# A decoder trunk on one core: the weights of the MLPs' first products at 32 different offsets, in two buffers of their own

## The chip, the cores and the metric

The kernel runs on one core of one Trainium2 chip, as one program. The time is device microseconds of that core, the median of several executions. Five engines work side by side and meet through semaphores: TensorE (matrix products; PE in the profile, with PEld for the loading of its stationary operand), VectorE (DVE), ScalarE (ACT), GpSimd (POOL) and SyncE (SP, which issues most DMAs). A core's SBUF has 128 partitions, and an address below is a byte offset within one partition.

## The reference, cut to what matters

The program is a two-layer decoder trunk over 256 tokens with a width of 2048, in float32. Both layers have the same MLP and the same gated embedding behind it; the mixers differ (a gated delta rule in layer 0, differential attention in layer 1):

```python
for i in range(DEPTH):                                   # DEPTH = 2
    xn = rmsnorm(h, norm_mix[i])
    h = h + (gated_deltanet(xn, ...) if i < N_A else diff_attention(xn, k_shared, v_shared, ...))
    hn = rmsnorm(h, norm_mlp[i])
    h = h + jnp.square(jax.nn.relu(hn @ mlp_w1[i])) @ mlp_w2[i]      # 2048 x 8192, 8192 x 2048
    gate = jax.nn.sigmoid(rmsnorm(h, norm_ple[i]) @ ple_w_gate[i])
    h = h + (p[i] @ ple_w_proj[i]) * gate
    if i == N_A - 1:
        kv = rmsnorm(h, kv_norm) @ w_kv                  # shared keys and values
return rmsnorm(h, final_norm)
```

The change touches `hn @ mlp_w1[i]`, the first product of each MLP, and where the last norm keeps its result.

## The kernel before, in words

Every large product is made of three matmuls in place of one: the weights are split into a rounded part `hi` and a rest `lo`, the activations into `xh` and `xl`, and `hi*xh + hi*xl + lo*xh` is accumulated in PSUM.

**A chunk of weights.** `chunk` (line 117) loads 1 MB of weights, four blocks of 128 x 512, into a buffer `raw` (three of them) by one DMA of SP's queue. It then makes two half chunks of 1024 columns each: ScalarE casts `raw` to `hi` (line 131), VectorE subtracts `hi` from `raw` to get `lo` (line 132). `hi` and `lo` come from the pool `whl`, three buffers of each, 4096 bytes long, called `whi` and `wlo`. All products of the kernel share them in turn.

**Two ways to multiply.** `g1` (line 155) holds the activations still and streams 512 columns of weights past them, lines 166 to 168. `g2` (line 137) holds a 128 x 128 block of weights still and streams all 256 tokens past it, lines 150 to 152, which leaves the result transposed. A half chunk is 24 matmuls in `g2`, and a panel (512 columns of the product, eight half chunks) is 192.

**The MLP.** `mlp` (line 558) first transposes the stream (`transposed`, line 185: TensorE transposes, ScalarE writes `xh`, VectorE `xl`). Then `first(q)`, for q from 0 to 3, makes four panels with `g2`, and squares their positive part into `hidh` and `hidl` (lines 574 to 579: two halves of a panel, each an activation and a cast on ScalarE, a product and a difference on VectorE). `second(q)` multiplies these with the second weights by `g1` and adds the result to the stream. The order is first(0), first(1), second(0), first(2), second(1), first(3), second(2), second(3). Per layer that makes 16 panels of `g2`, 32 in both.

**The order of the work.** The framework plans each engine's queue when the program is built: each engine takes its instructions in one fixed order, and an instruction may be moved ahead of others where its operands are there earlier. A write into a buffer that comes round again waits for the buffer's last readers.

**Where things lie.** A pool gives its tiles addresses in the order in which their names first occur. In the kernel before, all `whi` and `wlo` begin at a multiple of 512 bytes. The activations have one tile each for `xh` and `xl`, 16896 bytes, and `xpair` (line 200) gives two views of it: `xa` begins 448 bytes past a multiple of 512 (SHIFT = 112 floats) and `xs` at the multiple itself. `g2` streams `xa` (in attention `xb`, with the same shift). The operands that `g1` holds still are `xs` (gated embedding) and `oT` (attention's output, line 717), both at a multiple of 512, `hidh` and `hidl` at 256 past it, `oh` and `ol` (the delta rule's output, line 514) at 384 past it, and `xa` at 448 past it. The pool of an MLP, `ffn0` or `ffn1`, opens at address 122112, which is 256 past a multiple of 512, with two `hidh` and two `hidl` of 16384 bytes each. It lies over the memory of the mixer's pools, which are closed by then; 187648 and on was `R1`, `o` and `kT` of the delta rule.

Of the kernel before, what the change touches and what calls it, by code (L numbers as in the profile page):

```python
# [10 lines left out]
F32 = mybir.dt.float32  # L11
F32R = mybir.dt.float32r
# [4 lines left out]
P = 128  # L17
D = 2048
T = 256
NT = T // P  # L20
KD = D // P
# [16 lines left out]
class Trunk:  # L38
# [75 lines left out]
        self.w_gdn = self.cols[:, 112:113]  # L114
        self.w_sub = self.cols[:, 113:115]

    def chunk(self, src, kn, cols):

        nc = self.nc
        raw = self.wraw.tile([P, 2048], F32, name="raw")  # L120
        size = kn * cols
        nc.sync.dma_start(out=raw[:, :size].rearrange("p (k n) -> p k n", k=kn),
                          in_=src.rearrange("(k p) n -> p k n", p=P))
        res = []
        step = 1024 // cols
        for k0 in range(0, kn, step):
            kk = min(step, kn - k0)
            sl = raw[:, k0 * cols:(k0 + kk) * cols]
            hi = self.whl.tile([P, 1024], F32R, name="whi")[:, :kk * cols]
            lo = self.whl.tile([P, 1024], F32R, name="wlo")[:, :kk * cols]  # L130
            nc.scalar.copy(hi, sl)  # L131
            nc.vector.tensor_tensor(lo, sl, hi.bitcast(F32), ALU.subtract)  # L132
            res.append((hi.rearrange("p (k n) -> p k n", k=kk),
                        lo.rearrange("p (k n) -> p k n", k=kk), k0, kk))
        return res

    def g2(self, x, w, nk, c0, cols, kn):

        nc = self.nc
        xh, xl = x  # L140
        nct = cols // P
        banks = [self.bank() for _ in range((nct + 1) // 2)]
        for kb in range(0, nk, kn):
            for hi, lo, k0, kk in self.chunk(w[kb * P:(kb + kn) * P, c0:c0 + cols], kn, cols):
                for k in range(kk):
                    kt = kb + k0 + k
                    for ct in range(nct):
                        o = banks[ct // 2][:, (ct % 2) * T:(ct % 2) * T + T]
                        cs = slice(ct * P, ct * P + P)
                        nc.tensor.matmul(o, hi[:, k, cs], xh[:, kt], start=kt == 0 and ct % 2 == 0, stop=False, skip_group_check=True)  # L150
                        nc.tensor.matmul(o, hi[:, k, cs], xl[:, kt], start=False, stop=False, skip_group_check=True)  # L151
                        nc.tensor.matmul(o, lo[:, k, cs], xh[:, kt], start=False, stop=kt == nk - 1, skip_group_check=True)  # L152
        return banks
# [404 lines left out]
    def mlp(self, h, layer, w, pool):  # L558
        nc, d = self.nc, self.d
        w1, w2 = d["mlp_w1"][layer], d["mlp_w2"][layer]  # L560
        self.transposed(h, [(self.xa, w)])
        r = self.rstd(h)
        r2 = self.small.tile([P, NT], F32, name="r2")
        nc.vector.tensor_tensor(r2, r, r, ALU.mult)

        def first(q):
            hh = pool.tile([P, KD, T], F32R, name="hidh")
            hl = pool.tile([P, KD, T], F32R, name="hidl")
            for nb in range(4):
                for b, bk in enumerate(self.g2(self.xa, w1, KD, q * D + nb * 512, 512, 4)):  # L570
                    k = nb * 4 + 2 * b
                    a = pool.tile([P, 512], F32, name="relu")
                    s = pool.tile([P, 512], F32, name="relu2")
                    nc.scalar.activation(a, bk, AF.Relu)
                    nc.vector.tensor_tensor(s, a, a, ALU.mult)
                    fh = hh[:, k:k + 2].rearrange("p a b -> p (a b)")
                    fl = hl[:, k:k + 2].rearrange("p a b -> p (a b)")
                    nc.scalar.copy(fh, s)
                    nc.vector.tensor_tensor(fl, s, fh.bitcast(F32), ALU.subtract)
            return hh, hl  # L580

        def second(q, hid):
            for nb in range(4):
                bk = self.g1(hid, w2[q * D:(q + 1) * D], KD, nb * 512)
                for t in range(NT):
                    s = h[t][nb]
                    nc.vector.scalar_tensor_tensor(s, bk[t], r2[:, t:t + 1], s, ALU.mult, ALU.add)

        prev = first(0)
        for q in range(1, 4):  # L590
            cur = first(q)
            second(q - 1, prev)
            prev = cur
        second(3, prev)
# [127 lines left out]
    def final(self, h, pool):  # L722
        nc = self.nc
        fw = pool.tile([P, D], F32, name="hidl")
        nc.gpsimd.dma_start(out=fw, in_=self.d["final_norm"].partition_broadcast(P))
        y = [[pool.tile([P, 512], F32, name=f"y{t}{b}", bufs=1) for b in range(4)] for t in range(NT)]
        for b in range(4):
            for t in range(NT):
                nc.vector.tensor_tensor(y[t][b], h[t][b], fw[:, b * 512:(b + 1) * 512], ALU.mult)
        r = self.rstd(h)  # L730
        for t in range(NT):
            for b in range(4):
                if b % 2 == 0:
                    nc.scalar.activation(y[t][b], y[t][b], AF.Copy, scale=r[:, t:t + 1])
                else:
                    nc.vector.tensor_scalar(y[t][b], y[t][b], r[:, t:t + 1], None, ALU.mult)
                nc.sync.dma_start(out=self.out[0, t * P:(t + 1) * P, b * 512:(b + 1) * 512], in_=y[t][b])
# [55 lines left out]
```

## Time and profile before

| | |
|---|---|
| median of 3 runs | 2949.67 us (2949.06 to 2953.2) |
| the profiled execution: its own time | 2951.79 us |
| its span, first to last instruction | 2950.0 us |
| granted TensorE clock, mean over the span | 0.996 of full speed |
| TensorE busy (matmul) | 2909.7 us, 99% |
| weight loads busy | 2626.2 us, 89% |
| VectorE busy | 1782.8 us, 60% |
| ScalarE busy | 1451.8 us, 49% |
| moved by DMA | 527 MB, 179 GB/s |

Busy time counts an engine from the start to the end of each instruction. Matmuls overlap: the next one starts before the last has ended, so a busy share of 99% says that TensorE hardly ever waits, not that it streams at its best. How fast it goes is read from the distance between the starts of two matmuls, or from a stretch divided by the number of matmuls in it. The wait views name, for each instruction, what its engine waited for and how long; a chain view follows the work that ended last back from the end.

### The profile page before, as it was taken

The page shows a single profiled execution, that of the slowest core. Times are in us where ns is not written, and L with a number is a line of the kernel's source. Part 1 is how long each engine was busy: PE and PEld are TensorE (multiplying, and loading weights), DVE is VectorE, ACT ScalarE, POOL GpSimd, SP SyncE. Part 2 cuts the span into 40 slices and gives each one's busy share as a digit, 9 for nine tenths or more (in the row PEclk, how much of TensorE's full clock was granted, in tenths as well). Part 3 has the DMA queues.
Part 4 walks back from the last instruction along what each step waited for, and adds up shares of the span by engine and source line. Part 5 has one row for each costly group of instructions (what it writes and reads, how often), then busy time and mean ns, then how long its engine had stood idle before and what let it go on. Part 6 is the DMA issues. An engine that isn't in the chain of part 4 may idle for free.

```text
span 2950.0 us, 44777 instructions
## 1 busy us (share of the span) xinstructions
PE 2909.7 (99%) x18730; PEld 2626.2 (89%) x18730; DVE 1782.8 (60%) x2324; ACT 1451.8 (49%) x1947; POOL 60.4 (2%) x64
## 2 busy tenths in 40 slices
PE   8999999999999999999999999999999999999998
PEld 8989889988988998989988889987899899898886
DVE  7879766666666555555555565567555555555565
ACT  5655555545545443444434553367544444344454
POOL 1011000000000000000000000000000000000000
PEclk9999999999999999999999999999999999999999
DMA  6654544455445665655565556654566565556654
GB/s 200 207 168 140 175 161 138 149 175 161 133 143 182 194 196 190 188 194 189 186 198 189 178 170 198 191 166 144 183 192 197 189 192 192 188 186 198 202 172 155
DMA packets 289595, 527.19 MB, mean 179 GB/s; under 512 B 25966, under 2 KB 44560, under 8 KB 289264
## 3 DMA queue, kind: packets, MB, share of 16 engines
q1 hardware_dynamic: 288160, 521.77, 55.3%
q8 instruction: 147, 2.41, 0.3%
q0 software_dynamic: 816, 2.03, 0.2%
q10 hardware_dynamic: 416, 0.53, 0.1%
q14 instruction: 56, 0.46, 0.0%
HBM read 520.03 MB, written 4.26 MB: 178 GB/s over the span
## 4 chain that ended last, share of the span: by engine, by line
PE 93%; DVE 4%; ACT 2%; DMA 0%; issue 0%; POOL 0%; ACTq 0%; DVEq 0%
PE accb L166 16%; PE accb L167 16%; PE accb L168 16%; PE accb L151 13%; PE accb L152 13%; PE accb L150 13%; PE misb L429 2%; DVE wlo L132 1%; ACT whi L131 1%; PE misb L434 1%; PE misb L412 0%; PE misb L444 0%; PE misb L193 0%; PE misb L421 0%; DMA h<-x 0%
## 5 line engine op out<-in xcount | busy, mean ns | idle before, releaser
L132 DVE TENSOR_TENSOR wlo<-raw,whi 128x1024 fp32r<-128x1024 f32 x970 | 1190.1, 1228 | 985.0 <-ACT whi L131 983.6
L131 ACT CAST whi<-raw 128x1024 fp32r<-128x1024 f32 x970 | 1019.2, 1051 | 1296.8 <-PE accb L168 677.5
L150 PE MATMUL accb<-xha,whi 128*128 128x256 f32 x3344 | 939.4, 281 | 0.8 <-ACT whi L131 0.8
L151 PE MATMUL accb<-xla,whi 128*128 128x256 f32 x3344 | 937.6, 280 | 1.6 <-DVE xla L198 1.6
L152 PE MATMUL accb<-xha,wlo 128*128 128x256 f32 x3344 | 936.9, 280 | 0.5 <-DVE wlo L132 0.5
L152 PEld LDWEIGHTS accb<-xha,wlo 128*128 128x128 f32 x3344 | 633.2, 189 | 0.7 <-DVE wlo L132 0.7
L151 PEld LDWEIGHTS accb<-xla,whi 128*128 128x128 f32 x3344 | 629.7, 188 | 2.4 <-DVE xla L198 2.2
L150 PEld LDWEIGHTS accb<-xha,whi 128*128 128x128 f32 x3344 | 630.4, 189 | 1.4 <-ACT whi L131 1.0
L168 PE MATMUL accb<-whi,hidl 128*128 128x512 f32 x1024 | 398.5, 389 | 0.0
L167 PE MATMUL accb<-wlo,hidh 128*128 128x512 f32 x1024 | 398.5, 389 | 0.0
L166 PE MATMUL accb<-whi,hidh 128*128 128x512 f32 x1024 | 398.5, 389 | 0.0
L166 PE MATMUL accb<-whi,xha 128*128 128x512 f32 x640 | 254.2, 398 | 1.2 <-ACT xha L197 1.2
L167 PE MATMUL accb<-wlo,xha 128*128 128x512 f32 x640 | 252.8, 395 | 0.1
L168 PE MATMUL accb<-whi,xla 128*128 128x512 f32 x640 | 251.9, 394 | 0.0
L168 PEld LDWEIGHTS accb<-whi,hidl 128*128 128x128 f32 x1024 | 192.3, 188 | 40.1
L166 PEld LDWEIGHTS accb<-whi,hidh 128*128 128x128 f32 x1024 | 192.3, 188 | 39.9
L167 PEld LDWEIGHTS accb<-wlo,hidh 128*128 128x128 f32 x1024 | 192.3, 188 | 39.1
L166 PEld LDWEIGHTS accb<-whi,xha 128*128 128x128 f32 x640 | 120.4, 188 | 26.2 <-ACT xha L197 2.5
L167 PEld LDWEIGHTS accb<-wlo,xha 128*128 128x128 f32 x640 | 120.5, 188 | 25.0 <-DVE wlo L132 1.4
L168 PEld LDWEIGHTS accb<-whi,xla 128*128 128x128 f32 x640 | 120.3, 188 | 24.2
L166 PE MATMUL accb<-whi,oh 128*128 128x512 f32 x256 | 101.1, 395 | 0.8 <-ACT oh L469 0.8
L167 PE MATMUL accb<-wlo,oh 128*128 128x512 f32 x256 | 101.1, 395 | 0.0
(276 smaller groups left out, 2616.5 us busy)
## 6 DMA issues: line engine op xcount, KB each, us to landing
raw<-mlp_w SPq DMA_DIRECT2D x256, 1024.0 KB, 5.2
raw<-gdn_w_in SPq DMA_DIRECT2D x97, 1024.0 KB, 5.1
raw<-gdn_w_out SPq DMA_DIRECT2D x32, 1024.0 KB, 5.0
raw<-ple_w_gate SPq DMA_DIRECT2D x32, 1024.0 KB, 5.0
raw<-w_kv SPq DMA_DIRECT2D x32, 1024.0 KB, 5.2
raw<-diff_w_q SPq DMA_DIRECT2D x16, 1024.0 KB, 5.0
raw<-diff_w_o SPq DMA_DIRECT2D x16, 1024.0 KB, 5.0
gcb<-gcd SPq DMA_DIRECT2D x16, 256.0 KB, 4.3
```

Source lines behind the costliest of these rows:

```text
L131: nc.scalar.copy(hi, sl)
L132: nc.vector.tensor_tensor(lo, sl, hi.bitcast(F32), ALU.subtract)
L150: nc.tensor.matmul(o, hi[:, k, cs], xh[:, kt], start=kt == 0 and ct % 2 == 0, stop=False, skip_group_check=True)
L151: nc.tensor.matmul(o, hi[:, k, cs], xl[:, kt], start=False, stop=False, skip_group_check=True)
L152: nc.tensor.matmul(o, lo[:, k, cs], xh[:, kt], start=False, stop=kt == nk - 1, skip_group_check=True)
L166: nc.tensor.matmul(banks[t], xh[:, kt, ts], hi[:, k], start=kt == 0, stop=False)
L167: nc.tensor.matmul(banks[t], xh[:, kt, ts], lo[:, k], start=False, stop=False)
L168: nc.tensor.matmul(banks[t], xl[:, kt, ts], hi[:, k], start=False, stop=kt == nk - 1)
L429: nc.tensor.matmul(ps[:, h * P:(h + 1) * P], NTt[:, 2 * h + c], X[:, h * P:(h + 1) * P], start=True, stop=True)
L434: nc.tensor.matmul(ps[:, h * P:(h + 1) * P], UB[:, 2 * h + c], X[:, h * P:(h + 1) * P], start=True, stop=True)
```

## The change

The 32 panels of the MLPs' first products no longer take `whi` and `wlo` from the shared pool. `g2` and `chunk` get a further argument, `place`: a pool and an offset in floats. With it, `hi` and `lo` are tiles `vhi` and `vlo` of the MLP's own pool, two buffers of each in place of three, 1152 floats (4608 bytes, nine times 512) long, of which 1024 are used from the offset on. The offset is 8 floats, 32 bytes, times a number from 0 to 15: the panel's index in layer 0, and five times the index plus three, modulo 16, in layer 1. To make room, the last norm's eight tiles `y` become slices of one tile that takes a buffer of `hidh`. Nothing else is edited: the amount of work, its DMAs and its matmuls are the same.

```diff
-    def chunk(self, src, kn, cols):
+    def chunk(self, src, kn, cols, place=None):
...
-            hi = self.whl.tile([P, 1024], F32R, name="whi")[:, :kk * cols]
-            lo = self.whl.tile([P, 1024], F32R, name="wlo")[:, :kk * cols]
+            if place:
+                pool, off = place
+                hi, lo = (pool.tile([P, 1152], F32R, name=n, bufs=2)[:, off:off + kk * cols] for n in ("vhi", "vlo"))
+            else:
+                hi, lo = (self.whl.tile([P, 1024], F32R, name=n)[:, :kk * cols] for n in ("whi", "wlo"))
...
-    def g2(self, x, w, nk, c0, cols, kn):
+    def g2(self, x, w, nk, c0, cols, kn, place=None):
...
-            for hi, lo, k0, kk in self.chunk(w[kb * P:(kb + kn) * P, c0:c0 + cols], kn, cols):
+            for hi, lo, k0, kk in self.chunk(w[kb * P:(kb + kn) * P, c0:c0 + cols], kn, cols, place):
...
             for nb in range(4):
-                for b, bk in enumerate(self.g2(self.xa, w1, KD, q * D + nb * 512, 512, 4)):
+                i = 4 * q + nb
+                off = 8 * ((5 * i + 3) % 16 if layer else i)
+                for b, bk in enumerate(self.g2(self.xa, w1, KD, q * D + nb * 512, 512, 4, (pool, off))):
...
-        y = [[pool.tile([P, 512], F32, name=f"y{t}{b}", bufs=1) for b in range(4)] for t in range(NT)]
+        ys = pool.tile([P, 2 * D], F32, name="hidh")
+        y = [[ys[:, (4 * t + b) * 512:(4 * t + b + 1) * 512] for b in range(4)] for t in range(NT)]
```

## Rows read from the trace of the kernel before

**Rows 1.** The page: span, busy time by engine, and the chain by engine.
```profile
span 2950.0 us, 44777 instructions
PE 2909.7 (99%) x18730; PEld 2626.2 (89%) x18730; DVE 1782.8 (60%) x2324; ACT 1451.8 (49%) x1947; POOL 60.4 (2%) x64
...
PE 93%; DVE 4%; ACT 2%; DMA 0%; issue 0%; POOL 0%; ACTq 0%; DVEq 0%
```
**Rows 2.** First products by stretch: bounds, length, busy PE PEld DVE ACT POOL, clock.
```profile
931.60:1102.80 171.20, 171.20 (x1513) 171.20 (x1512) 97.05 (x99) 82.55 (x96) 0.00 (x0) 1.00 0.61 191
1189.90:1280.30 90.40, 90.40 (x769) 90.38 (x768) 47.85 (x46) 40.34 (x45) 0.00 (x0) 1.00 0.59 187
1367.40:1457.80 90.40, 90.40 (x769) 90.39 (x768) 47.85 (x46) 40.35 (x45) 0.00 (x0) 1.00 0.59 187
2133.20:2304.40 171.20, 171.20 (x1513) 171.20 (x1512) 97.03 (x99) 82.55 (x96) 0.00 (x0) 1.00 0.61 191
```
**Rows 3.** Stretches of g1: `hid`, `oT`, `xa`, `oh` held still; columns as above.
```profile
1105.00:1185.00 80.00, 80.00 (x355) 66.27 (x354) 41.56 (x39) 31.45 (x32) 0.00 (x0) 1.00 0.60 194
2062.00:2120.00 58.00, 58.00 (x258) 48.04 (x257) 30.56 (x28) 27.14 (x34) 0.00 (x0) 1.00 0.60 194
1925.30:1941.30 16.00, 16.00 (x71) 13.15 (x70) 6.88 (x7) 6.32 (x6) 0.00 (x0) 1.00 0.62 194
902.00:922.00 20.00, 20.00 (x87) 16.21 (x86) 12.55 (x15) 10.92 (x20) 0.00 (x0) 1.00 0.56 181
```
**Rows 4.** TensorE in order of time at a panel's end: start, length, line.
```profile
1059.34 0.28 PE L150 MATMUL accb<-xha,whi 128*128 128x256 f32 x1
...
1062.06 0.28 PE L150 MATMUL accb<-xha,whi 128*128 128x256 f32 x1
...
1062.29 0.28 PE L152 MATMUL accb<-xha,wlo 128*128 128x256 f32 x1
```
**Rows 5.** ScalarE there, idle time ahead of an instruction in brackets.
```profile
1058.86 0.60 ACT L574 ACTIVATE relu<-accb 128x512 f32<-128x512 f32 x1 [1.10 <-PE accb L152]
1059.43 1.06 ACT L131 CAST whi<-raw 128x1024 fp32r<-128x1024 f32 x1
...
1060.90 0.59 ACT L574 ACTIVATE relu<-accb 128x512 f32<-128x512 f32 x1
1062.20 1.05 ACT L131 CAST whi<-raw 128x1024 fp32r<-128x1024 f32 x1 [0.71 <-PE accb L151]
```
**Rows 6.** VectorE there.
```profile
1060.52 1.23 DVE L132 TENSOR_TENSOR wlo<-raw,whi 128x1024 fp32r<-128x1024 f32 x1 [0.33 <-ACT whi L131]
```
**Rows 7.** GpSimd at the opening of the first MLP's pool.
```profile
924.82 1.13 POOL L600 DMA_DIRECT2D p<-p  x2 [145.61 <-PE misb L193]
```
**Rows 8.** Instructions on `kT`, 600 to 930 us: durations, first and last start.
```profile
L393 PE MATMUL misb<-q,kT x12: 275/275/276, 642.6 to 860.1; 128*128 128x128 f32 x12
```
**Rows 9.** ScalarE from the last output product into the first MLP.
```profile
918.72 1.05 ACT L131 CAST whi<-raw 128x1024 fp32r<-128x1024 f32 x1 [1.74 <-PE accb L168]
...
921.51 1.05 ACT L131 CAST whi<-raw 128x1024 fp32r<-128x1024 f32 x1 [0.37 <-PE accb L168]
924.29 1.05 ACT L131 CAST whi<-raw 128x1024 fp32r<-128x1024 f32 x1 [1.73 <-PE accb L168]
925.24 1.56 ACT L197 ACTIVATE xha<-misb,cols 128x256 fp32r<-128x256 f32 x4
```
**Rows 10.** TensorE there.
```profile
924.09 1.91 PE L193 MATMUL misb<-ident,h 128*128 128x128 f32 x16
925.76 0.50 PE L150 MATMUL accb<-xha,whi 128*128 128x256 f32 x2
927.04 0.39 PE L151 MATMUL accb<-xla,whi 128*128 128x256 f32 x1 [0.78 <-DVE xla L198]
...
928.53 1.47 PE L193 MATMUL misb<-ident,h 128*128 128x128 f32 x12
929.76 0.36 PE L151 MATMUL accb<-xla,whi 128*128 128x256 f32 x1
```

## The prediction

> **What bounds the kernel now.** I read the page first: TensorE is busy for 99% of the span and the chain that ended last is TensorE for 93% [rows 1]. So a wait of another engine matters only where it makes TensorE stop, and the time can change in two ways: by the pace at which TensorE goes through its matmuls, or by new stops. The second view is the busy time by stretch [rows 2]. In the first products TensorE's busy time equals each stretch's length; there are no stops. But the pace differs. In the stretch of first(0) and first(1), 171.20 us hold 1512 matmuls (the count less the one in flight at its start), 113.2 ns each. In first(2) and in first(3), 90.40 us hold 768, 117.7 ns each. The granted clock is 1.00 in all, the shapes, the lines and the buffers are the same, and layer 1 repeats it: four stretches of four panels are slow (two stand in the rows), 16 panels of 32, or 3072 matmuls. At 4.5 ns each the slow ones lose 13.8 us. Within a stretch the pace never changes. It is fast where the stretch is entered from the transposes and slow where it is entered from a product of g1.
>
> The third view is the same for g1, where the operand that is held still lies at several distances from the streamed one [rows 3]. Less the one or two in flight, the spacings are 226.6 ns with `hid` (256 bytes past a multiple of 512, streamed weights at 0), 226.6 with `oT` (0), 228.6 with `xa` (448) and 232.6 with `oh` (384). A matmul of g1 needs 512 columns and one weight load, one of g2 256 columns and one weight load, and 226.6 is twice 113.3. So I read one and the same floor in both, and an excess for each weight load that goes with the distance between the two operands modulo 512: 0 at 0 and 256, 2.0 ns at 448, 6.0 ns at 384, and in g2, where the held weights are at 0 and the stream at 448 (a distance of 64), 0 or 4.5 ns by the way in.
>
> **The change part by part.**
>
> *The offsets.* Ahead of `vhi` the MLP's pool holds two `hidh` and two `hidl` of 16384 bytes each and starts 256 past a multiple of 512, so `vhi` and `vlo` start there too. With the stream at 448, a panel with the offset b bytes has the distance b + 320 modulo 512. The 16 offsets take each multiple of 32 once in each layer; the present distance of 64 comes with b = 256, in one panel per layer. No row shows g2 at another distance. From both sides: if every distance is fast, the 13.8 us are gained; if every one is as bad as `oh`, 6144 matmuls lose 6.0 ns, 36.9 us, which is 23.1 more than now. Between, I take the mean of the five positions shown, (0 + 0 + 2.0 + 6.0 + 2.25) / 5 = 2.05 ns, where 2.25 is half of 4.5: 6144 x 2.05 = 12.6 us against the 13.8 of now, so 1.2 us less. The nearest row is the kernel's own half-and-half, and this value lies next to it.
>
> On the offsets the Trainium skill speaks against the change doing anything. The spread of rows 2 and 3 at one clock is what the trace shows. TensorE: Matmul & The Clock Gate, section "Step-by-step: what each phase is for", says that TensorE has two independent read ports into SBUF, so that loading the next weights takes nothing from the running matmul; SBUF — State Buffer, section "Who interferes with whom", adds that TensorE waits on nobody. By it the distance would cost nothing; the rows agree for `hid` and `oT` and differ by 6.0 ns for `oh`. What would be left is the way in, which is a rival below.
>
> *Two buffers in place of three, in the steady run.* At a panel's end the next panel's first matmul starts at 1059.34 and its second half chunk at 1062.06 [rows 4]. The cast that starts at 1059.43 waits for the buffer that was just freed [rows 5]. With three buffers it is for the half chunk after next; with two it feeds the one at 1062.06. Its `lo` is done at 1060.52 + 1.23 = 1061.75 [rows 6], and the first matmul on `lo` starts at 1062.29, whose weights are loaded during the matmul before, so from 1062.18: 0.43 us to spare. At the next boundary the cast starts at 1062.20, 0.14 behind the half chunk's start, and the same sum leaves 0.4. The cast needs ScalarE for 1.05 us and `lo` needs VectorE for 1.23 of the 2.72 us of a half chunk, and the squaring of the panel fits into the gaps as it does now. I cost it at nothing; if the planner puts the second relu of a panel (0.59 us, at 1060.90) ahead of that cast, the cover is gone and TensorE stops for some 0.2 us, and with the cast of `hidh` as well for 0.8. The extreme is 32 panels at 0.8, 26 us; a gain is excluded, since TensorE has no stop there. Both transfers of a chunk keep their three `raw` buffers and come a half chunk later at the same distance from each other: nothing.
>
> *The way into the MLP.* Now the casts for the first three half chunks start at 918.72, 921.51 and 924.29, before the transposes give the first operand [rows 9]. `vhi` lies in memory of the mixer's closed pools. The trace shows how such a first write waits: GpSimd's load of `p`, in the same pool, waits until TensorE's transposes, 924.82 [rows 7], though `kT`, over which it lies, is last read at 860.1 [rows 8]. So I expect the first cast at about 924.3, behind the last output product, and two of the three casts move into the stretch in which ScalarE and VectorE make `xa`. Queued behind the waiting cast on ScalarE are the first `xha`, which wait for the transposes anyhow and now also start behind a cast, at 925.24 [rows 9]. The first products at 925.76 stay; TensorE's present stop until 927.04 hides the first `lo`. The second half chunk is wanted at 929.76 [rows 10]; its cast and `lo` (1.05 + 1.23 us) must be fitted between the `xha` and the transposes in front of it hide part. Bounds per layer: nothing, or both casts and both `lo` in the open, 2 x (1.05 + 1.23) = 4.6 us. I take 1.5, as the transposes (1.47 us at 928.53) give cover for the rest; for two layers 3.0, ends 0 and 9.
>
> *Between first and second.* Each kind has buffers of its own, so casts can run ahead across the change. TensorE has no stop there now: nothing to gain, and none to lose while ScalarE is half idle.
>
> *The last norm.* `ys` takes the buffer of `hidh` that `first(2)` filled, whose reader `second(2)` ends long before the last norm. Its slices are written as separate regions, as the slices of `xha` are, which TensorE reads while ScalarE still writes others [rows 9, 10]: nothing.
>
> **Sum.** Against the profiled execution's own 2951.8 us (1.8 around the span): -1.2 + 3.0 gives 2953.6. The median of the runs is 2.1 below that execution; from it the sum is 2951.5. I say 2953.
>
> **The rivals.**
> *The way in decides, not the distance.* For: one and the same distance runs at both paces in rows 2. Against: `oh` is slow over its whole stretch and `oT` is not. The offsets then change nothing and 3.0 us of the way in remain: 2953.
> *Most distances slip* (the other side). Place: the weight load beside the stream, in the panels away from 0 and 256. Price: as for `oh`, 6.0 ns a matmul. If three quarters of the panels do so, 4608 x 6.0 = 27.6, less 13.8, plus 3.0: 2967. It decides from the point where more than 20 of the 32 panels slip so (20 x 192 x 6.0 = 23.0, with 3.0 more a loss of 12). Half the positions seen have an excess, and the present distance was fast at least half of the time.
> *Most distances are fast.* For: two of the four distances of g1 are at the floor. All fast: 2950.5 - 13.8 + 3.0 = 2940; three quarters fast and the rest as now: 2944.
> *The two buffers are one too few.* The Trainium skill, Perfetto Trace Analysis, section "Optimization Strategy", says that the same gap again and again on the engine that should be saturated can mean too few buffers; no run here shows it yet. The price comes from the cast and the relu above: 0.4 us in each of 32 panels, 13 us: 2966. For: only 0.43 us to spare. Against: the order of rows 5 already puts the cast ahead of the second relu.
>
> **How the numbers follow.** The forecast of mixed paces has 0.42, the way in 0.08, most slip 0.22, most fast 0.16, two buffers 0.12. A change below 0.2% of the time, 5.9 us, can't be told from none. Mixed paces end within it for the greater part, with some on both sides; the way in does; most fast ends faster, the other two slower. That gives 0.21 faster, 0.40 within, 0.39 slower. The range leaves out the far half of "most slip" and of "most fast": 2940 to 2968. The forecast's own range is 2945 to 2960.
>
> **What would show it.** In the changed trace the panels' lengths, 192 matmuls each: 21.7 us at the floor, 22.6 at the present slow pace, 22.9 at the pace of `oh`; the step holds if several lengths stand beside each other and go with the distance in both layers, though their order differs. Equal lengths in all panels, or lengths that go with q as now, would refute the distance. Idle time ahead of line 152 with `vlo` at each panel's end would show the two buffers, idle time between 927 and 934 us the way in. The sum is wrong if the mean excess of the 32 panels is outside 1 to 4 ns.

## The result, and the profile after

The changed kernel took 2976.09 us (median of three runs, 2974.96 to 2983.52) against 2949.67 us: a ratio of 1.0093, with a 95% interval of 1.0065 to 1.0121. That is 26.4 us slower, above the predicted range. The profiled execution took 2983.52 us itself, with a span of 2981.7 us, 31.7 more than in [rows 1].

The page of the changed kernel, the lines that answer to [rows 1]: the span, busy time by engine, the chain's shares by engine.

```profile
span 2981.7 us, 44745 instructions
PE 2935.5 (98%) x18730; PEld 2649.0 (89%) x18730; DVE 1782.1 (60%) x2324; ACT 1452.0 (49%) x1947; POOL 60.7 (2%) x64
...
PE 89%; DVE 5%; ACT 3%; DMA 2%; issue 1%; POOL 0%; ACTq 0%; SPq 0%; DVEq 0%
```

TensorE has as many matmuls as before and is busy 25.8 us longer: the same work goes more slowly. The span has grown by 31.7 us, more than the busy time, and so has the share of the chain that is not TensorE's: there are new stops as well. Both stand in the panels. Busy time in stretches of one panel each, answering to [rows 2]; the columns are bounds, length, busy time and count by engine, clock, DMA share and GB/s, all engines in the first three rows, TensorE alone in the last three:

```profile
952.11:975.16 23.05, 23.05 (x195) 23.05 (x193) 12.30 (x12) 10.55 (x13) 0.00 (x0) 1.00 0.60 188
975.16:997.94 22.78, 22.78 (x195) 22.78 (x193) 12.30 (x12) 10.52 (x13) 0.00 (x0) 1.00 0.60 184
1020.97:1043.59 22.62, 22.62 (x195) 22.62 (x193) 12.30 (x12) 10.52 (x13) 0.00 (x0) 1.00 0.58 184
...
2175.69:2197.49 21.80, 21.80 (x194) 1.00 0.60 186
2242.67:2265.39 22.72, 22.72 (x195) 1.00 0.61 186
2467.20:2489.60 22.40, 22.40 (x195) 1.00 0.59 188
```

Six panels of the same 192 matmuls, all without a stop and at a granted clock of 1.00, take 21.80 to 23.05 us. The table has every panel that is neither the first after the transposes nor ended by a stop (a length is from the start of a panel's first matmul to the start of the next panel's). Distance is the start of the held operand less that of the streamed one, modulo 512 bytes; two distances 256 apart share a row.

| Distance | layer 0, us | layer 1, us |
|---|---|---|
| 0, 256 | 23.04, 23.04 | (both with stops) |
| 32, 288 | (both with stops) | 22.71, 22.71 |
| 64, 320 | 22.62 | 21.80, 22.61 |
| 96, 352 | 22.53, 23.04 | 22.79, 22.79 |
| 128, 384 | 22.79, 22.78 | 22.78 |
| 160, 416 | 23.04 | 23.04 |
| 192, 448 | 22.62, 22.61 | 22.61, 22.61 |
| 224, 480 | 22.61, 22.61 | 22.40, 22.40 |

Only one panel of the 24 comes to the floor of 21.76, and it has a distance of 64, which the kernel before had in all of them; the other panel at 64, entered from g1, takes 22.62. Of the two panels left out at the heads of the layers, the one at 320 runs at 113.3 ns behind its last stop, the one at 416 at 119.9. Less the stops and the way in, the spacings of the 6144 matmuls average 118.6 in layer 0 and 118.3 in layer 1, against a floor of 113.3 ns: an excess of some 5.1 ns.

The stops stand where first products end. The changed kernel around the end of first(1): TensorE, ScalarE, VectorE by time; start, length, line, and in brackets the idle time ahead and what ended it.

```profile
1106.75 0.39 PE L153 MATMUL accb<-xha,vhi 128*128 128x256 f32 x1 [0.31 <-ACT vhi L134]
...
1108.38 0.39 PE L155 MATMUL accb<-xha,vlo 128*128 128x256 f32 x1 [1.13 <-DVE vlo L135]
```
```profile
1103.75 2.00 ACT L134 CAST whi<-raw 128x1024 fp32r<-128x1024 f32 x2 [2.01 <-DMA raw<-mlp_w]
1105.65 2.00 ACT L134 CAST vhi<-raw 128x1024 fp32r<-128x1024 f32 x2
```
```profile
1104.83 2.36 DVE L135 TENSOR_TENSOR wlo<-raw,whi 128x1024 fp32r<-128x1024 f32 x2 [1.83 <-ACT whi L134]
1107.11 2.36 DVE L135 TENSOR_TENSOR vlo<-raw,vhi 128x1024 fp32r<-128x1024 f32 x2
```

ScalarE's queue has the two casts for the second products (`whi`) ahead of the last two for the panel that TensorE is in (`vhi`). The buffers of `whi` are free, so the order planned when the program is built lets them go first; but their data isn't there, and ScalarE waits 2.01 us for that transfer while TensorE runs out of `vhi` and `vlo`. Six stretches of first products end in this way: spacings of over 350 ns sum to 4.8 us there in layer 0 and 2.1 in layer 1.

The panel's end inside a stretch, which answers to [rows 5, 6], keeps its cover and its order: ScalarE takes the first cast, then the cast of `hidh` and the second relu, then the second cast, and TensorE has no gap.

```profile
1066.28 1.05 ACT L134 CAST vhi<-raw 128x1024 fp32r<-128x1024 f32 x1
1067.24 0.61 ACT L583 CAST hidh<-relu 128x512 fp32r<-128x512 f32 x1
1067.75 0.59 ACT L579 ACTIVATE relu<-accb 128x512 f32<-128x512 f32 x1
1069.21 1.05 ACT L134 CAST vhi<-raw 128x1024 fp32r<-128x1024 f32 x1 [0.86 <-ACT relu L579]
```

The way in, answering to [rows 9, 10], ScalarE and then TensorE:

```profile
924.46 1.05 ACT L134 CAST vhi<-raw 128x1024 fp32r<-128x1024 f32 x1 [3.92 <-issue]
925.41 1.56 ACT L200 ACTIVATE xha<-misb,cols 128x256 fp32r<-128x256 f32 x4
...
929.15 1.07 ACT L134 CAST vhi<-raw 128x1024 fp32r<-128x1024 f32 x1
```
```profile
923.99 0.39 PE L171 MATMUL accb<-whi,ol 128*128 128x512 f32 x1
924.22 1.91 PE L196 MATMUL misb<-ident,h 128*128 128x128 f32 x16
925.93 0.50 PE L153 MATMUL accb<-xha,vhi 128*128 128x256 f32 x2
927.21 0.39 PE L154 MATMUL accb<-xla,vhi 128*128 128x256 f32 x1 [0.78 <-DVE xla L201]
```

The first cast starts at 924.46, behind the last output product, and the second at 929.15. From the last output matmul to the second panel's first matmul it is 28.12 us in layer 0, 26.68 before. In layer 1 the same way costs 1.41 us more than before in the kernel of the first experiment below, whose pace there is that of before.

A last part lies where the change touches nothing. The attention stage of layer 1 has eight panels of the same form, at a distance of 64. The changed kernel, then the kernel before, in the same 45 us:

```profile
1775.00:1820.00 45.00, 45.00 (x384) 45.00 (x384) 22.23 (x20) 16.67 (x17) 0.00 (x0) 1.00 0.62 203
```
```profile
1775.00:1820.00 45.00, 45.00 (x400) 45.00 (x399) 23.06 (x21) 16.94 (x17) 0.00 (x0) 1.00 0.60 199
```

The 384 and the 400 matmuls, less one in flight, are 117.5 and 112.8 ns each. That stage is 6.8 us longer in the profiled execution, the slowest of the three; the other two runs were 7.4 and 8.6 us faster than it. So of the 31.7 us of the profiled execution 14.4 are in layer 0's MLP, 10.4 in layer 1's and 6.8 in the attention stage, and the 26.4 us between the medians are near the 24.8 of the MLPs alone. Of those, some 17.5 are pace, 6.1 the stops (6.9 less the spacing that these matmuls have anyway) and 2.9 the way in; 1.7 come back, since the work behind the last first product is 0.85 us shorter in each layer. Together that is the 24.8.

### The profile page after: what moved, and what is told of

Its sections match the earlier page's. It is cut to its first block, busy times and chain, and to the rows that moved or that the text cites. A ratio compares the mean times of both kernels' runs of the same rounds, so it can differ in the third digit from the quotient of the medians.

```text
span 2981.7 us, 44745 instructions
## 1 busy us (share of the span) xinstructions
PE 2935.5 (98%) x18730; PEld 2649.0 (89%) x18730; DVE 1782.1 (60%) x2324; ACT 1452.0 (49%) x1947; POOL 60.7 (2%) x64
## 4 chain that ended last, share of the span: by engine, by line
PE 89%; DVE 5%; ACT 3%; DMA 2%; issue 1%; POOL 0%; ACTq 0%; SPq 0%; DVEq 0%
PE accb L170 16%; PE accb L169 15%; PE accb L171 15%; PE accb L155 12%; PE accb L154 12%; PE accb L153 12%; DVE wlo L135 2%; PE misb L432 2%; DMA raw<-mlp_w 1%; ACT whi L134 1%; DVE vlo L135 1%; ACT xha L200 1%; PE misb L415 1%; PE misb L437 1%; ACT vhi L134 0%
## 5 line engine op out<-in xcount | busy, mean ns | idle before, releaser
L155 PE MATMUL accb<-xha,vlo 128*128 128x256 f32 x2048 | 575.3, 281 | 5.4 <-DVE vlo L135 5.4
L154 PE MATMUL accb<-xla,vhi 128*128 128x256 f32 x2048 | 575.2, 281 | 1.5 <-DVE xla L201 1.5
L153 PE MATMUL accb<-xha,vhi 128*128 128x256 f32 x2048 | 574.8, 281 | 0.3 <-ACT vhi L134 0.3
L155 PEld LDWEIGHTS accb<-xha,vlo 128*128 128x128 f32 x2048 | 386.4, 189 | 7.4 <-DVE vlo L135 7.1
L154 PEld LDWEIGHTS accb<-xla,vhi 128*128 128x128 f32 x2048 | 385.7, 188 | 2.1 <-DVE xla L201 2.0
L153 PEld LDWEIGHTS accb<-xha,vhi 128*128 128x128 f32 x2048 | 385.7, 188 | 1.1 <-ACT vhi L134 0.8
L153 PE MATMUL accb<-xha,whi 128*128 128x256 f32 x1296 | 369.4, 285 | 0.8 <-ACT whi L134 0.8
L155 PE MATMUL accb<-xha,wlo 128*128 128x256 f32 x1296 | 367.0, 284 | 0.5 <-DVE wlo L135 0.5
L154 PE MATMUL accb<-xla,whi 128*128 128x256 f32 x1296 | 367.2, 283 | 0.2 <-DVE xla L201 0.2
L155 PEld LDWEIGHTS accb<-xha,wlo 128*128 128x128 f32 x1296 | 244.8, 189 | 0.7 <-DVE wlo L135 0.7
```

## Experiments

Thirteen kernels were run beside the two. The theory at the outset: the distance of held and streamed operand sets the pace, most distances are worse than 64, and the buffers of their own cost the rest. The rivals: the work ahead of a stretch sets the pace, and two buffers are one too few.

**1. The buffers without the offsets.** All panels at a distance of 64.

```
-                off = 8 * ((5 * i + 3) % 16 if layer else i)
+                off = 64
```

> The changed kernel with one offset, 256 bytes, for all 32 panels: the distance between held weights and stream is that of the kernel before, 64; the two buffers of their own stay. If the distance sets the pace, panels take 21.8 or 22.6 us as before, and only the stops at the ends of the six stretches stay (about 1.2 us each, 7 us in all): 2953 to 2960 us. If the buffers or their place make the loss, panels stay at 22.6 to 23.0 us: 2970 us or more.

Measured: 2962.53 us, ratio 1.0041 (1.0022 to 1.0059). Layer 0's first panels, and its waits of TensorE from 931 to 1470 us (releaser: total, times, longest):

```profile
955.00:1095.00 140.00, 140.00 (x1238) 1.00 0.62 193
```
```profile
PE accb L155 <- DVE vlo L135: 3.8, 4, 1.1
```

The panels are back at 113.2 ns (140.00 / 1237) in the stretches that come from the transposes, 21.76 us each, and at 22.61 in those that come from g1, exactly as before. So the offsets did the slowing of the pace: 13.6 us between the two medians, 15.4 in the MLPs of the two traces. The stops at the stretches' ends and the way in stay and belong to the buffers. The time lies 2.5 us above the range expected, and the eight runs span 16 us.

This trace also shows where a pace changes. TensorE at the end of first(2) in layer 0, from the last panel's first matmul to its last; every panel here has a distance of 64:

```profile
1259.33 0.28 PE L153 MATMUL accb<-xha,vhi 128*128 128x256 f32 x1
...
1276.17 0.28 PE L155 MATMUL accb<-xha,vlo 128*128 128x256 f32 x1
...
1278.23 0.39 PE L155 MATMUL accb<-xha,vlo 128*128 128x256 f32 x1 [1.13 <-DVE vlo L135]
1278.45 0.28 PE L153 MATMUL accb<-xha,vhi 128*128 128x256 f32 x1
...
1283.45 0.28 PE L155 MATMUL accb<-xha,vlo 128*128 128x256 f32 x1
```

The 143 spacings ahead of the stops are 117.8 ns each, the 44 behind them 113.6. Of the six stretches' ends four change their pace so, three from 118 to 114 and one from 113 to 118, and two keep it.

**2. The distance without the buffers.** The kernel before, its streamed operand moved by 64 bytes, so that every first product has a distance of 0.

```
-SHIFT = 112
+SHIFT = 128
```

> The kernel before with its three shared buffers, and xa 64 bytes further on, so that the distance in every g2 is 0. If the distance sets the pace, every MLP panel takes 23.0 us, as the panels at distances 0 and 256 of the changed kernel (27 us more in the MLPs), the panels of attention and of the delta rule go the same way, and g1 with xa held still drops from 228.6 to 226.6 ns a matmul: 2980 to 2995 us. If the buffers make the loss, or the way in alone sets the pace, the MLP panels stay at 21.8 and 22.6 us: 2945 to 2952 us.

Measured: 2994.75 us, ratio 1.0139 (1.0121 to 1.0156). Every panel without a stop, of both MLPs and of attention, takes 23.04 us (a few 23.03), whichever way it is entered:

```profile
960.00:1110.00 150.00, 150.00 (x1252) 1.00 0.58 183
```

119.9 ns with the three shared buffers: at this distance the place of the operands alone costs what the table shows at 0 and 256. (The 41 us are more than the MLPs' 27, since the edit moves every product that streams or holds `xa` or `xb`.)

**3. Offsets in steps of 4 bytes.** Distances of 32 to 92 in the changed kernel.

```
-                off = 8 * ((5 * i + 3) % 16 if layer else i)
+                off = 56 + ((5 * i + 3) % 16 if layer else i)
```

> The changed kernel with 16 offsets in steps of 4 bytes instead of 32, distances 32 to 92, each once a layer. If the pace goes with the distance, panels of one distance take about the same time in both layers, 21.8 or 22.6 us at 64 and 22.5 to 23.0 at 32 and at 92; the steps between say how wide the place of the floor is. If only multiples of 32 bytes count, those between fall together with their neighbours. A theory of buffers alone expects one length for all.

Measured in a single run: 2979.39 us. Three panels: distance 52 in layer 0; 76, entered from g1, and 52 in layer 1:

```profile
1041.25:1063.04 21.79, 21.79 (x195) 1.00 0.61 190
2419.93:2441.70 21.77, 21.77 (x193) 1.00 0.42 127
2464.42:2486.18 21.76, 21.76 (x194) 1.00 0.61 189
```

The floor showed at 52 in both layers and at 76 and 88 in one each (their other panel ends in a stop); both panels at 64 took 22.62, the rest without a stop 22.61 to 23.04. So a step of 4 bytes already tells, and 76 held where 64 had not: entered from g1.

**4. Another way in.** The kernel before, with two transposes on TensorE ahead of first(2) and first(3).

```
+            if q > 1:
+                kick = self.bank(2 * P, self.mis)
+                for t in range(NT):
+                    nc.tensor.transpose(kick[:, t * P:(t + 1) * P], self.ident, self.ident)
```

> The kernel before, with two transposes of a constant (four passes) on TensorE ahead of first(2) and of first(3) in both layers; nothing reads them. If the way in decides between the two paces at distance 64, and transposes lead into the fast one, the 16 slow panels drop from 22.6 to 21.8 us, 13.6 us less, for about 2 us of transposes: 2938 us. If the slow pace belongs to these panels for another reason, 2 us are lost: 2952 us.

Measured: 2955.06 us, ratio 1.0004 (0.9992 to 1.0016). The panels behind the transposes stay at 117.4 ns (60.00 / 511):

```profile
1215.00:1275.00 60.00, 60.00 (x512) 1.00 0.59 187
```

A miss. A stretch entered from the MLP's own transposes is fast, but two transposes by themselves don't make one fast. They came without a stop of TensorE, while in the MLP's own way in TensorE stops (0.78 us at 927.04 [rows 10]). In the twelve traces with one distance for all first products, experiment 13's left out, no unbroken run of 60 or more of them changes its pace by more than 0.4 ns (means of 24 matmuls): every change stands behind a stop, as in experiment 1, or behind other products. Whether a stop by itself changes the pace, and what chooses the new one, no run tests.

**5 to 7. The three good distances, reached by moving the stream.** The kernel before, with `SHIFT = 109`, `115` and `106`: distances 76, 52 and 88, by another start of the streamed operand.

> The kernel before with its shared buffers and xa 436 instead of 448 bytes past a multiple of 512, so that every g2 has the distance 76. In the scan of 4-byte steps the two panels at 76 ran at the floor, one of them entered straight from g1. If the distance alone decides there, all 32 MLP panels take 21.8 us (13.6 us less), attention's 8 panels are at the floor in every execution, and g1 with xa held moves by -2 to +4 ns a matmul (1152 matmuls, -2 to +5 us): 2932 to 2945 us. If the floor at 76 needs a certain way in, first(2) and first(3) stay at 22.6 us and more: 2948 us or above.

> As the run at distance 76, with xa at 460 bytes, distance 52 in every g2, whose two panels of the scan were at the floor, both entered from a panel of g2 and none from g1. Distance alone: 2932 to 2945 us, all MLP panels 21.8. Way in: the stretches entered from g1 at 22.6 us or more, 2948 us or above.

> As before at distance 88 (xa at 424 bytes), where both panels of the scan were at the floor, entered from panels of g2. Distance alone: 2932 to 2945 us. Way in: 2948 us or above.

Measured: 3000.55 (ratio 1.0159, 1.0139 to 1.0179), 2979.01 (1.0086, 1.0067 to 1.0105) and 2998.04 us (1.0149, 1.0131 to 1.0167). First products of layer 0 in the three, in this order:

```profile
970.00:1120.00 150.00, 150.00 (x1252) 1.00 0.58 183
```
```profile
960.00:1110.00 150.00, 150.00 (x1282) 1.00 0.59 185
```
```profile
965.00:1115.00 150.00, 150.00 (x1255) 1.00 0.58 183
```

119.9, 117.1 and 119.6 ns: none is fast. In the second kernel layer 1's first stretch, first(0) and first(1), runs slower still, at 23.04 us a panel against 22.50 in the MLPs' other panels, and in the first kernel attention's panels take 23.68. The theory that the distance alone decides fell here. In steps of 32 bytes of the held operand it orders the panels; in steps of 4 bytes it matters which of the two operands was moved. A rival is left: the stream's own start, which is off a multiple of 64 bytes in these three kernels and on one in all the fast ones, may cost by itself.

**8. Both products in the MLP's buffers.** Experiment 1, with the second products' casts in the same two buffers.

```
...
-                bk = self.g1(hid, w2[q * D:(q + 1) * D], KD, nb * 512)
+                bk = self.g1(hid, w2[q * D:(q + 1) * D], KD, nb * 512, place=(pool, 64))
```

> The changed kernel with the one offset of 256 bytes, in which second() takes the two buffers of the MLP's pool as well, so that its casts can no longer run ahead of those of first(). If the stops at the ends of the six stretches come from casts that ran ahead across the two kinds of buffers, they go: panels 21.8 and 22.6 us, the last ones too, 8 us less than with the second product on the shared buffers, 2950 to 2954 us. If two buffers by themselves are too few, the stops stay or spread to the ends of other panels: 2958 us or more.

Measured: 2957.64 us, ratio 1.0014 (1.0000 to 1.0027). Waits of TensorE from 931 to 1470 us:

```profile
PE accb L155 <- DVE vlo L135: 0.5, 1, 0.5
```

The one wait left is in the way in. The stops at the ends are gone and the last panels are at 21.76 and 22.61 us. With one kind of buffer a cast can't overtake across kinds, and two buffers are enough. So the stops came from the two kinds beside each other, not from the number. The time lies 3.6 us above the range expected; in the profiled execution attention's panels run at the slower of their two paces, which is worth 8 x 0.85 = 6.8.

**9, 10. Distance 76 and 52 for all first products**, in the kernel of experiment 8; the held operand moves and the stream stays. The edit is that of experiment 9, and 61 stands for 67 in experiment 10.

```
-                off = 64
+                off = 67
```

> Both products of the MLPs take their weights from the two buffers of their own, so that no cast runs ahead across two kinds of buffers; the first products' weights stand 268 bytes in (distance 76 to the streamed operand, which stays where it was), the second products' 256 bytes in. Theory A (the distance, with the streamed operand on its old start, sets the pace, and 76 is fast whichever work comes before): all 32 panels at 21.8 us in place of 16 at 22.6; 16 x 0.85 = 13.6 us under the two-buffer kernel at distance 64: about 2944 with the attention at its slower pace, 2937 with its faster one. Rival B (what comes ahead decides at 76 as at 64; the fast panel seen at 76 had its luck from the panel before): the stretches entered from second products stay at 22.6 us, 2957 in all. Rival C (76 was fast only because the panels beside it had other distances): all at 22.4 to 23.0, 2960 to 2970.

> The same with the weights of the first products 244 bytes in (distance 52). In the scan by steps of 4 bytes a panel at 52 was at 21.8 us in both layers, while the same distance reached by moving the streamed operand ran at 22.5. Theory A (the held operand's own place counts, with the stream on its old start): 32 panels at 21.8 us, about 2944 or 2937. Rival B (the work ahead decides): 16 at 21.8 and 16 at 22.6, about 2957. Rival C: all at 22.5 as with the moved stream, 2970.

Measured at 76: 2941.61 us, ratio 0.9943 (0.9927 to 0.996). The four stretches that had been slow in the kernel before:

```profile
1190.00:1275.00 85.00, 85.00 (x753) 1.00 0.61 191
1365.00:1450.00 85.00, 85.00 (x753) 1.00 0.61 192
2392.00:2475.00 83.00, 83.00 (x735) 1.00 0.61 192
2566.00:2650.00 84.00, 84.00 (x743) 1.00 0.60 192
```

85.00 / 752 is 113.0 ns. All 32 panels are at the floor, in the first of each layer the 138 spacings behind its last stop; by 16 x 0.85 that is 13.6 us better than experiment 8. Between the two medians lie 16.0 us, by the two ratios some 21; both hold the change of attention's pace from run to run. At 52: 2944.06 us, ratio 0.9964 (0.9946 to 0.9982), with ten runs from 2935.94 to 2955.68. In the profiled one, layer 0's first stretch and layer 1's:

```profile
975.00:1100.00 125.00, 125.00 (x1106) 1.00 0.62 194
2160.00:2310.00 150.00, 150.00 (x1252) 1.00 0.58 184
```

113.1 against 119.9 ns at the same addresses. So 52 too has two paces, and 8 panels at 23.04 in place of 21.76 are 10.2 us: that the median is the 2944 expected for one fast pace is luck. At 76 all panels behind the first of a layer had one pace in the three profiles taken, but the other pace shows in the way in. Experiment 9, ahead of a stop and at its end (four transposes of `p` lie between the last two lines):

```profile
930.23 0.28 PE L153 MATMUL accb<-xha,vhi 128*128 128x256 f32 x1
...
932.39 0.29 PE L154 MATMUL accb<-xla,vhi 128*128 128x256 f32 x1
...
933.45 0.39 PE L155 MATMUL accb<-xha,vlo 128*128 128x256 f32 x1 [0.34 <-DVE vlo L135]
```

The 18 spacings between the first two lines are 120.0 ns each, those behind the third 113.5 on average.

**11. The same cause in g1.** The kernel before, with 128 unused bytes ahead of `oh` and `ol`.

```
+            one.tile([P, 32], F32, name="pad")
             self.cw = one.tile([P, 4, 64], F32, name="cw")
```

> The kernel before with 128 unused bytes ahead of the tiles oh and ol, so that the held operand of the eight output projections of the first attention stage starts on a multiple of 256 bytes in place of 128 past one. Nothing else of it moves but the buffers behind. Theory A (the 232 ns of these 96 matmuls each, against 226.6 of the MLPs' second products, are the distance of held and streamed operand, 384 modulo 512): they fall to 226.6 to 227 ns, 8 x 96 x 5.7 ns = 4.4 us less in the span, verdict within 2949 to 2946. Rival B (that stage has other work on the PE's path and it gives the time back): the rows go to 227 and the total stays. Rival C (their excess has another cause, such as what is read beside them): 232 ns stay.

Measured: 2948.50 us, ratio 0.9979 (0.9968 to 0.999). The last output product, answering to the fourth of [rows 3]:

```profile
898.00:915.00 17.00, 17.00 (x77) 1.00 0.60 184
```

17.00 / 75 (two in flight) is 226.7 ns, 232.6 before. What the prediction had read from that row, an excess that goes with the distance, held for g1 at the one distance tried.

**12, 13. Both edits, and attention at 76 too.** Experiment 9 with the pad; then also the query and key weights of the attention stage, in the tiles that hold the values later.

```
+                if off < 0:
+                    self.turn = 1 - self.turn
+                    pair = pool.tile([P, D + 128], F32, name=f"v{self.turn}")[:, 67:67 + D].bitcast(F32R)
+                    hi, lo = pair[:, :kk * cols], pair[:, 1024:1024 + kk * cols]
...
-                    for b, bk in enumerate(self.g2(x, w, KD, nb * 512, 512, 4)):
+                    for b, bk in enumerate(self.g2(x, w, KD, nb * 512, 512, 4, (one, -1))):
```

> The kernel with both MLP products in the two buffers of their own and distance 76 for the first products, and the 128 unused bytes ahead of oh and ol: two edits that were timed apart (ratios 0.9943 and 0.9979). Theory A (each acts on its own rows of the PE's chain): their product, 0.992, some 23 us under the kernel before, MLP panels at 21.8 us and output projections at 227 ns. Rival B (shared slack: one gives back what the other gains): no better than 0.994.

> The same, and the eight panels of the second attention stage that multiply by the query and key weights get their weights at distance 76 too, in the two tiles that hold the values later. The bytes, products and sums are those of the kernel before. Theory A (at distance 64 what comes ahead decides whether these eight panels run at 21.8 or 22.6 us, and so from one execution to the next; at 76 nothing does): 8 panels at 21.8 us in every execution, so up to 6.8 us less and a narrower spread of the times than before's 13 us, less 1 to 3 us for a stop at their end, where the values' weights go back to the three shared buffers and their casts run ahead. Rival B (the spread has another source, such as the transfers): the spread stays as wide, 8 to 13 us, though the panels are at 21.8. Rival C (76 holds only in the MLPs): 22.4 us or more, nothing gained and the stop lost.

Measured: 2938.01 us, ratio 0.9938 (0.9923 to 0.9953), and 2943.07 us, ratio 0.9955 (0.9942 to 0.9967). The first is the fastest kernel of this study, 20.1 us under the runs of the kernel before beside it, and some 46 us under the changed one by the two ratios (0.0155 of 2950). Its rows show both gains, panels at 21.76 us and output products at 226.8 ns, but its ratio lies between the 0.992 expected if both add up and the 0.994 of shared slack, and its interval overlaps that of experiment 9: that the two gains add up in full isn't shown. In the second the attention panels run at 113.2 ns (140.00 / 1237), and its six runs span 5.3 us, where those of the first span 9.4 and ten of the kernel before 9.5; with the two paces of attention in the profiles that makes the panels at 64 a likely source of the spread. But it loses more at its edges, some 10 us in the profiled executions, than the 6.8 it can gain. The entry to that stage, then its panels:

```profile
1725.00:1730.00 5.00, 0.16 (x1) 0.19 (x2) 4.50 (x11) 5.00 (x15) 3.25 (x8) 0.75 0.51 54
1730.00:1735.00 5.00, 3.88 (x17) 3.32 (x16) 4.73 (x14) 4.97 (x11) 0.00 (x0) 0.50 0.00 0
...
1750.00:1890.00 140.00, 140.00 (x1238) 1.00 0.60 196
```

TensorE is busy for 0.16 of 5 us, and the granted clock is 0.75 there and 0.50 behind it, which is 1.2 of 2.4 GHz; in the kernel of experiment 12 TensorE is busy for 3.18 us in those 5 and the clock stays at 1.00. I had counted the stop at the other end (2.1 us measured) and not this one. The clock can fall at this entry without the edit too. The kernel before, where TensorE was busy for 3.42 us in the 5 ahead:

```profile
1740.00:1745.00 5.00, 4.61 (x28) 4.29 (x28) 4.78 (x13) 4.63 (x13) 2.04 (x6) 0.66 0.56 69
```

## Why the prediction was wrong, step by step

**The pace, and what bounds the kernel:** right. TensorE's pace decided, the clock was 1.00 in every panel of the MLPs, and 26 us came without any other engine becoming the bound.

**The offsets:** the step that failed, by its size. The prediction put "the mean of the five positions shown" at 2.05 ns and came to 1.2 us less than before; measured was an excess of some 5.1 ns, and the step's part is some 17 us more. The mechanism was right in part: panels of several lengths beside each other, alike in both layers in three of the six rows of the table that have both. What failed is carrying the costs from g1 to g2. The prediction counted 0 and 256 as free and 448 as 2.0 ns, from `oT`, `hid` and `xa`, which are operands of g1. In g2 the table and experiment 2 give 6.7 ns at 0 and 256, 4.5 at 448 and 5.3 at 384; with these values and the same 2.25 at 64 the same mean comes to 5.1. What a distance costs in g1 doesn't carry to g2. Nor was the 2.0 a fixed cost in g1: the product with `xa` that the prediction read at 228.6 ns goes at 233.4 in the changed kernel (96 matmuls from 1941.2 us on), whose attention ran at its slower pace just ahead. And the present distance, taken for a middling one, is one of the few that reach the floor at all: of the eight rows of the table only its own does. The mean excess lies outside the 1 to 4 ns beyond which the prediction called its sum wrong.

**The rival "most distances slip":** this is what came. Its point was "more than 20 of the 32 panels", and its price 6.0 ns; of the 24 panels in the table 23 slip, by 3.3 to 6.7 ns. Its 2967 fell short of 2976 by the stops and because more than three quarters slip.

**The Trainium skill's rule** that TensorE reads SBUF through two independent ports (TensorE: Matmul & The Clock Gate, "Step-by-step: what each phase is for") would leave the pace the same at every offset. Experiment 2 moves one operand by 64 bytes and gives 119.9 in place of 113.2 and 117.7 ns: here the measurement decides against it. What makes the difference, no run shows.

**Two buffers in the steady run:** right. Behind the way in no panel inside a stretch has a stop, and experiment 8 runs every panel as before with two buffers. The Trainium skill's reading of gaps that return again and again as too few buffers (Perfetto Trace Analysis, "Optimization Strategy") would have misled at the stretches' ends: there the gaps went away with the number of buffers unchanged.

**"Between first and second":** the second step that failed. The text said that casts can run ahead across the change, and put that at "nothing to gain, and none to lose while ScalarE is half idle". They do run ahead, and that is the loss, some 6 us: ScalarE is half idle but takes its queue in order, and a cast that is early waits for a transfer that isn't there yet.

**The way into the MLP:** right, 2.9 us against 3.0: 1.44 in layer 0 and 1.41 in layer 1. The first cast came at 924.46 where 924.3 had been said.

**The last norm:** nothing showed. Behind the last first product each layer's rest is 0.85 us shorter, not longer, than before.

**The rival "the way in decides":** half right. It doesn't decide at 0 (experiment 2), nor between the two ways into a stretch at 76 (experiment 9). But at 64 and 52 the same addresses run at two paces, experiment 4 says that not any transposes will do, and in experiment 1 the pace changed at a stop with nothing but first products around it. The table has one or two panels to a distance, so how much of its order is the distance and how much the way in stays open.

## What to carry to other kernels

Where TensorE is the bound and has no stops, compare the spacing of its matmuls between stretches and on both sides of a stop, and try the start of the stationary operand against the moving one in small steps, one product form at a time: between good and bad lay 6% of an MLP panel here. Two kinds of buffers that follow each other on one in-order engine let casts of the later kind overtake the earlier ones; let consecutive products share one kind. And when a distance has been in use for long, ask first whether it is one of the few good ones: a scatter over all of them is a bet against it.

## What was not expected of the hardware

- The spacing of matmuls of 256 columns at one clock went from 113.3 to 120.0 ns (21.76 and 23.04 us a panel) with the start of the held operand alone, and a step of 4 bytes told. Moving the streamed operand to the same distance did not give the same pace (distance 76: 113.0 and 119.9 ns). Why is open.
- At distances of 64 and 52, and in the way in at 76, one and the same form at the same distance has two paces (113 and 118 ns at 64, 113 and 120 at the others). A pace holds, to 0.4 ns, while TensorE runs on with these products, and can be another behind a stop (117.8 and 113.6 in experiment 1). Attention's panels at 64 had the faster pace in the profiles of three kernels and the slower one in those of seven, with nothing changed in that stage.
- In g1 128 unused bytes ahead of `oh` took its matmuls from 232.6 to 226.7 ns; what is free in g1 (a distance of 0) is the worst in g2 (119.9 ns).
- At the entry to attention the granted clock fell to 0.50 in experiment 13, where TensorE had been busy for 0.16 of 5 us, and to 0.66 over 5 us in the kernel before; in experiment 12 it stayed at 1.00. ScalarE and VectorE were busy throughout.
